# Three modulation blocks moved to an earlier layer, two last taps and two group roots set ahead of weight splits, and small matrix products given other places

## The chip, the cores and the metric

The kernel runs on one core of one Trainium2 chip. The metric is the device time of one execution in microseconds (us). TensorE is called PE below, VectorE DVE, ScalarE ACT, GpSimd POOL and SyncE SP. Each engine takes its instructions strictly in the order in which they were written into its program, and waits at each one until the semaphores that it names have come.

## The reference

A two-layer "macaron" network with adaptive norms, one batch, 256 tokens, width 1024, all in float32. There are six sub-layers: feed-forward, hybrid mixer, feed-forward, then feed-forward, mLSTM, feed-forward. The change touches the first two. Each sub-layer gets a modulation (shift, scale and gate) that is a product of one conditioning vector with a large matrix:

```python
for layer in range(DEPTH):
    mod = (c_act @ ada_w[layer] + ada_b[layer]).reshape(bsz, N_SUB, 3, D_MODEL)[:, :, :, None, :]
    def modulate(t, sub):
        return rms_norm(t, norm_g[layer, sub]) * (1.0 + mod[:, sub, 1]) + mod[:, sub, 0]
    h = modulate(x, 0)
    x = x + HALF_STEP * (1.0 + mod[:, 0, 2]) * swiglu(h, ffn_w_gate[layer, 0], ...)
    h = modulate(x, 1)
    y = hybrid_mixer(h, ...)          # layer 0; layer 1 has the mLSTM here
    x = x + (1.0 + mod[:, 1, 2]) * y
    ...

def hybrid_mixer(h, w_in, w_out, ...):
    gate_lru, x_lru, z_ssd, xbc, dt_raw = jnp.split(h @ w_in, HYB_SPLITS, axis=-1)
    x_lru = causal_conv(x_lru, lru_conv_w, lru_conv_b)            # 4 taps
    y_lru = rg_lru(x_lru, ...) * jax.nn.gelu(gate_lru)
    xbc = jax.nn.silu(causal_conv(xbc, ssd_conv_w, ssd_conv_b))   # 4 taps
    ...
    y = ssd_chunked(xs, dt, a, bm, cm) + ssd_d[:, None] * xs
    y = y * jax.nn.silu(z_ssd)
    y = rms_norm(y in 2 groups of 512, ssd_norm_g)
    return jnp.concatenate([y_lru, y], axis=-1) @ w_out
```

## The kernel before, in words

**Weights in pieces.** All weight matrices stream through the core as one list of 128x128 tiles, eight to a piece of 512 KB. For each piece SP issues one DMA into one of four raw buffers (`wraw`, line 95). ACT rounds the piece to a high part (`whi`, line 101), and DVE subtracts that from the raw piece to get the low part (`wlo`, line 102, called the split below). PE then makes three products of each tile (high by high, high by low, low by high; lines 443 to 445, or 509 to 511 at the start of a sub-layer), 24 to a piece. These products are called stream products. The first feed-forward takes pieces 0 to 65, the hybrid mixer pieces 66 to 119, and four more sub-layers follow. Places within the hybrid are counted in stream products from piece 66 on: "at 788" means behind 788 of them.

**Modulation blocks.** The modulation of all sub-layers is 144 blocks of 512 KB (`ada`, line 262). Each is a DMA into one of three buffers and one multiply-and-accumulate on DVE. `ADA_PLAN` says in which sub-layer, and over which of its pieces, a range of blocks is spread evenly; 24 blocks belong to each sub-layer, in the order of the sub-layers, so blocks 24 to 47 are the hybrid's (40 to 47 its gate, used at its end).

**What sets the order.** The text of the program is written sub-layer by sub-layer. A list scheduler that works with costs of its own decides at build time in which order each engine gets its instructions, within the data dependencies and the buffer counts. Extra edges without a wait bind its choice: `W.behind(i, n, ins)` puts the ACT cast (n = 0) or the DVE split (n = 1) of piece i behind an instruction; `stand(ins, s, n)` puts a small PE product behind stream product n of sub-layer s; `in_one_go` ties products to each other; `issue_after` keeps everything in a block behind an instruction.

**The norm ahead of the hybrid (called n1).** Each 128-row slice of x is finished on DVE (line 571), squared on ACT (line 416), and the squares are summed over the rows by small PE products (`rst_n1`, line 359, at 11). DVE takes the reciprocal root in nine instructions on 128x2 numbers (`rsv`, `rsy`, `rsw`, lines 373 and 320 to 329), and two PE products spread it over all rows (`rsb_n1`, line 405, at 28). The first stream products of the sub-layer run on unnormalised rows meanwhile.

**The hybrid's own work.** Convolutions are one ACT instruction and three DVE taps (line 733), on `ssd_x` (from PE's `xbc`) and on `lru_x` (from PE's `xl`). Each `lru_x` slice is then split into a high part by ACT (line 426) and a low part by DVE (line 427), for the gate products `ri`. For each of four pairs of heads PE writes decay rows (`ab`, line 974), ACT makes from them `mt` (lines 983 and 986) and `ce` (line 985), DVE multiplies both with other matrices (lines 988 and 992), and PE makes y0, y2, y4 and y6 (line 1008). DVE and ACT scale and square y; after y2 and after y6 a group norm runs like the one above (`rst_g`, `rsv_g` to `rsy_g`, `rsb_g`; groups 0 and 1), and its result `ysb` is the input of the out products `od`. The `lru` scan (lines 1055 and 1057 on DVE) waits on a square root (line 1051) on ACT.

## Time and profile before

| what | value |
|---|---|
| three timed runs | 1096.56, 1097.56 and 1098.46 us (median 1097.56) |
| the profiled execution's own time | 1097.25 us |
| its span | 1095.5 us, so that 1.75 us lie around it |
| PE busy | 1083.8 us (99%) |
| DVE busy | 920.5 us (84%) |
| ACT busy | 639.5 us (58%) |
| DMA | 272.34 MB, mean 249 GB/s |
| first feed-forward | from the start to 193.7 us |
| hybrid | 193.7 to 367 us |

The rows of the timeline give start, duration, engine, line, operation, tiles out<-in and shapes, and in brackets the engine's idle time before the row with what ended it. A matmul's duration overlaps the next one's, so PE's pace is read from the distance of starts. Names in the rows leave out the buffer numbers.

### The profile page before, as it was taken

Reading aid. Unit: us, or ns where it says so; the run is one execution under the profiler, and the core shown is the slowest. Engines: PE = TensorE matmul, PEld = TensorE weight load, DVE = VectorE, ACT = ScalarE, POOL = GpSimd, SP = SyncE. Lnnn points to the kernel's source line nnn. Section 1 sums busy time; section 2 is a strip of 40 time slices with the busy share of each in tenths; the row PEclk is TensorE's granted clock in tenths of the full one; section 3 lists DMA queues with packets and bytes.
Section 4 is the critical chain, followed back from the end, with each engine's and each line's share of the span. In section 5 each row is a group of like instructions: output and inputs, shape, how many; then the busy total and the mean of one; then the engine's idle time right before and its main releaser. Section 6 shows DMA issues by size and latency. Waiting matters only on the chain.

```text
span 1095.5 us, 23272 instructions
## 1 busy us (share of the span) xinstructions
PE 1083.8 (99%) x9315; PEld 1070.4 (98%) x9315; DVE 920.5 (84%) x1654; ACT 639.5 (58%) x1053; POOL 8.8 (1%) x28
## 2 busy tenths in 40 slices
PE   9999999999999999999999999999999999999997
PEld 7999999999999999999999999999999999999997
DVE  7999999899999899989698798979768868866552
ACT  5765555678986564554454455448776655544452
POOL 0000000000000000000000000010000000000000
PEclk9999999999999999999999999999999999999999
DMA  9889999556855489999848799963432664875551
GB/s 375 344 318 391 387 352 343 178 196 195 279 167 191 139 307 370 354 351 327 281 142 323 266 356 346 338 204 119 146 102 81 208 193 137 298 239 193 193 174 39
DMA packets 75534, 272.34 MB, mean 249 GB/s; under 512 B 8593, under 2 KB 9393, under 8 KB 75426
## 3 DMA queue, kind: packets, MB, share of 16 engines
q1 hardware_dynamic: 74592, 269.38, 69.7%
q8 instruction: 73, 1.20, 0.4%
q0 software_dynamic: 400, 1.04, 0.4%
q10 hardware_dynamic: 434, 0.43, 0.1%
q14 instruction: 35, 0.29, 0.1%
HBM read 269.77 MB, written 1.05 MB: 247 GB/s over the span
## 4 chain that ended last, share of the span: by engine, by line
PE 80%; DVE 12%; DMA 4%; issue 2%; ACT 1%; ACTq 0%; DVEq 0%; SPq 0%
PE gu L445 12%; PE gu L444 12%; PE gu L443 11%; PE od L445 10%; PE od L443 10%; PE od L444 10%; DVE wlo L102 4%; DMA wraw<-in_wst_dram 3%; PE zz L445 1%; PE zz L443 1%; PE zz L444 1%; DMA wgr<-in_ml_wg_dram 1%; DVE ada L262 1%; DVE xc L733 1%; PE gu_f L509 1%
## 5 line engine op out<-in xcount | busy, mean ns | idle before, releaser
L102 DVE TENSOR_TENSOR wlo<-wraw,whi 128x1024 fp32r<-128x1024 f32 x364 | 442.9, 1221 | 83.6 <-ACT whi L101 83.0
L101 ACT CAST whi<-wraw 128x1024 fp32r<-128x1024 f32 x364 | 378.2, 1050 | 210.9 <-DMA wraw<-in_wst_dram 80.2
L444 PE MATMUL gu<-hb,whi 128*128 128x256 f32 x1296 | 358.0, 276 | 0.4 <-DVE hb L668 0.3
L443 PE MATMUL gu<-hb,whi 128*128 128x256 f32 x1296 | 358.0, 276 | 0.0
L445 PE MATMUL gu<-hb,wlo 128*128 128x256 f32 x1296 | 357.9, 276 | 0.1
L444 PEld LDWEIGHTS gu<-hb,whi 128*128 128x128 f32 x1296 | 243.3, 188 | 0.8 <-DVE hb L668 0.8
L445 PEld LDWEIGHTS gu<-hb,wlo 128*128 128x128 f32 x1296 | 243.3, 188 | 0.2 <-DVE wlo L102 0.2
L443 PEld LDWEIGHTS gu<-hb,whi 128*128 128x128 f32 x1296 | 243.2, 188 | 0.0
L443 PE MATMUL od<-ph,whi 128*128 128x256 f32 x704 | 194.3, 276 | 0.0
L444 PE MATMUL od<-ph,whi 128*128 128x256 f32 x704 | 194.3, 276 | 0.0
L445 PE MATMUL od<-ph,wlo 128*128 128x256 f32 x704 | 194.3, 276 | 0.0
L262 DVE SCALAR_TENSOR_TENSOR ada<-ada,cact 128x1024 f32<-128x1024 f32 x144 | 175.3, 1218 | 1.4 <-DMA ada<-in_adaT_dram 1.3
L444 PEld LDWEIGHTS od<-ph,whi 128*128 128x128 f32 x704 | 132.1, 188 | 0.0
L445 PEld LDWEIGHTS od<-ph,wlo 128*128 128x128 f32 x704 | 132.1, 188 | 0.0
L443 PEld LDWEIGHTS od<-ph,whi 128*128 128x128 f32 x704 | 132.1, 188 | 0.0
L426 ACT CAST ph<-fg 128x256 fp32r<-128x256 f32 x88 | 35.1, 406 | 114.9 <-DVE fg L595 114.9
L427 DVE TENSOR_TENSOR ph<-fg,ph 128x256 fp32r<-128x256 f32 x88 | 36.4, 421 | 14.2 <-ACT ph L426 14.2
L416 ACT ACTIVATE sq_o<-x 128x256 f32<-128x256 f32 x42 | 17.5, 418 | 45.6 <-DVE x L571 40.6
L571 DVE SCALAR_TENSOR_TENSOR x<-od,gate,x 128x256 f32<-128x256 f32 x48 | 23.1, 481 | 24.4 <-PE od L445 24.2
L444 PE MATMUL zz<-hb,whi 128*128 128x256 f32 x128 | 36.2, 283 | 0.0
L445 PE MATMUL zz<-hb,wlo 128*128 128x256 f32 x128 | 36.1, 282 | 0.0
L443 PE MATMUL zz<-hb,whi 128*128 128x256 f32 x128 | 35.8, 279 | 0.0
(431 smaller groups left out, 1959.1 us busy)
## 6 DMA issues: line engine op xcount, KB each, us to landing
wraw<-in_wst_dram SPq DMA_DIRECT2D x366, 512.0 KB, 4.6
ada<-in_adaT_dram SPq DMA_DIRECT2D x144, 512.0 KB, 5.6
xn<-in_x_dram SPq DMA_DIRECT2D x2, 512.0 KB, 4.0
wgr<-in_ml_wg_dram POOLq DMA_DIRECT2D x3, 256.0 KB, 5.4
...
```

Of the source, the lines that this page charges most:

```text
L101: raw_hi = nc.scalar.copy(hi, raw)
L102: self.last = nc.vector.tensor_tensor(out=lo, in0=raw, in1=hi.bitcast(F32), op=ALU.subtract)
L262: return nc.vector.scalar_tensor_tensor(out=raw, in0=raw, scalar=1.0, in1=cact, op0=ALU.mult, op1=ALU.mult, accum_out=mods[s][:, m:m + 1])
L416: square = nc.scalar.activation(q, x, AF.Square).ins
L426: nc.scalar.copy(hi, src)
L427: nc.vector.tensor_tensor(out=both[:, 1, :], in0=src, in1=hi.bitcast(F32), op=ALU.subtract)
L443: m = nc.tensor.matmul(dst, wh, both[:, 0, :], start=start, stop=False, skip_group_check=True)
L444: W.products += [m, nc.tensor.matmul(dst, wh, both[:, 1, :], start=False, stop=False, skip_group_check=True), nc.tensor.matmul(dst, wl, bo ...
L445: nc.tensor.matmul(dst, wl, both[:, 0, :], start=False, stop=stop, skip_group_check=True)]
L509: W.products += [nc.tensor.matmul(dst, wh, rh, start=(k == 0), stop=False), nc.tensor.matmul(dst, wh, rl, start=False, stop=False), nc.ten ...
L571: nc.vector.scalar_tensor_tensor(out=xs_t[d], in0=dst, scalar=g[:, d:d + 1], in1=xs_t[d], op0=ALU.mult, op1=ALU.add)
L733: nc.vector.scalar_tensor_tensor(out=dst[:, o:], in0=src[:, :T - o], scalar=cw(j), in1=dst[:, o:], op0=ALU.mult, op1=ALU.add)
```

## The change

The edits are these. (1) `ADA_PLAN`: blocks 40, 41 and 42 move from the hybrid to the first feed-forward, where blocks 16 and 17 now come at pieces 14 and 15, and blocks 18 to 42 (25 instead of 24) from piece 17 to 43; the hybrid keeps blocks 43 to 47, spread over its pieces 22 to 34. (2) The last tap of the first `ssd_x` slice is set ahead of the split of piece 75, and the last tap of the last `lru_x` slice ahead of the split of piece 97. (3) The end of the reciprocal root of group 0 is set ahead of the split of piece 105, that of group 1 ahead of that of piece 109; the scans come behind the root of group 1; the splits into `ysb0` to `ysb3` are written right behind group 0's norm. (4) y0 and y2 get places at 788 and 797, the sums of group 1 at 948 and their spread at 976; the n1 spread's place at 28 is written down, and 48 stream products are held behind the n1 sums and the n1 spread. No instruction is added or removed.

```diff
-SUMS = {"n1": (1, 11), "n2": (2, 11), "n4": (4, 14)}
+SUMS = {"n1": (1, 11), "n2": (2, 11), "n4": (4, 14), "g1": (1, 948)}
+KEPT, HELD = ("n1",), 48
+SPREADS = {"n1": (1, 28), "n2": (2, 28), "g1": (1, 976)}
...
 ADA_PLAN = [
-    (0, (17, 43), range(16, 40)), (0, (43, 65), range(48, 64)), (1, (22, 37), range(40, 48)),
+    (0, (14, 16), range(16, 18)), (0, (17, 43), range(18, 43)), (0, (43, 65), range(48, 64)),
+    (1, (22, 34), range(43, 48)),
     (2, (6, 60), range(64, 104)), (3, (6, 60), range(104, 136)), (5, (6, 40), range(136, 144)),
...
+    def hold(ins, s, n):
+
+        holds.append((ins, 3 * PIECE * starts[s] + n))
...
             if nm in SUMS:
                 stand(products[0], *SUMS[nm])
+                if nm in KEPT:
+                    hold(products[-1], *SUMS[nm])
...
-            if nm == "n2" and b == 0:
-                stand(m, 2, 28)
+            if b == 0 and nm in SPREADS:
+                stand(m, *SPREADS[nm])
+            if b == 1 and nm in KEPT:
+                hold(m, *SPREADS[nm])
...
+    taps = []
+
     def conv(dst, src, cw, cb, i, n):
...
-            nc.vector.scalar_tensor_tensor(out=dst[:, o:], in0=src[:, :T - o], scalar=cw(j), in1=dst[:, o:],
-                                           op0=ALU.mult, op1=ALU.add)
+            taps.append(nc.vector.scalar_tensor_tensor(out=dst[:, o:], in0=src[:, :T - o], scalar=cw(j),
+                                                       in1=dst[:, o:], op0=ALU.mult, op1=ALU.add))
...
                 xbc(xs[:, i, :], b[:, 0:T], i)
+                if i == 0:
+                    W.behind(starts[1] + 9, 1, taps[-1])
...
                 conv(xl[:, c, :], b[:, 0:T], lambda j: col("lru_cw", 8 * j + c), col("lru_cb", c), c, 8)
+                if c == 7:
+                    W.behind(starts[1] + 31, 1, taps[-1])
...
             in_one_go(products, needed)
+            if m0 < 4:
+                stand(products[0], 1, (788, 797)[m0 // 2])
...
                 if g == 0:
                     group_norm(0)
-        ys = [sp.tile([P, 2, T], F32R, tag=f"ssd{m % 4}{m // 4}", name=f"ysb{m}") for m in range(8)]
-        for m in range(4):
-            split(xs[:, m, :], ys[m])
+                W.behind(starts[1] + (39, 43)[g], 1, rsqrt_ends[-1])
+                ys += [sp.tile([P, 2, T], F32R, tag=f"ssd{m}{g}", name=f"ysb{4 * g + m}") for m in range(4)]
+                if g == 0:
+                    for m in range(4):
+                        split(xs[:, m, :], ys[m])
+        second_root = rsqrt_ends[-1]
...
-                nc.vector.tensor_tensor_scan(out=xl[:, c, :], data0=av[:, c, :], data1=nq[:, c, :], initial=0.0,
-                                             op0=ALU.mult, op1=ALU.add)
+                with tc.issue_after(second_root.ins):
+                    nc.vector.tensor_tensor_scan(out=xl[:, c, :], data0=av[:, c, :], data1=nq[:, c, :], initial=0.0,
+                                                 op0=ALU.mult, op1=ALU.add)
...
+    for i, n in holds:
+        for m in W.products[n:n + HELD]:
+            tc.add_manual_dep(m.ins, i.ins.name, NOSYNC, reason="not later")
```

The scheduler puts more in other places than the diff names. Three places follow, first of the kernel before, then of the changed one. In the changed kernel's rows the same source lines have numbers that are higher by 3 to 21. Numbers behind a name tell pieces and buffers (`wlo68` is piece 68); the last number is a serial one.

DVE where the first feed-forward ends and the hybrid begins, kernel before: `od0_7` is the last out product's bank, `rst_n1` the sum of the squares.

```order
L290 SCALAR_TENSOR_TENSOR scale2_4845<-scale2_4845,cols_104 128x8 [waits DVE_49]
L102 TENSOR_TENSOR wlo68_2546<-wraw68_2543,whi68_2545 128x1024 [waits DMAHW2_49,Activation_49]
L102 TENSOR_TENSOR wlo69_2576<-wraw69_2573,whi69_2575 128x1024 [waits DMAHW3_49,PE_49,Activation_49]
L571 SCALAR_TENSOR_TENSOR x_103<-od0_7_2524,gate0_1931,x_103 128x256 [waits PE_49]
L831 TENSOR_SCALAR dt_3168<-cols_104 128x8
L490 SCALAR_TENSOR_TENSOR hb_106<-x_103,scale1_1937,hb_106 128x256 [waits DVE_49,Activation_49]
L373 TENSOR_SCALAR rsv_n1_2636<-rst_n1_2631 128x2 [waits PE_49]
L320 TENSOR_SCALAR rsy_n1_2639<-rsv_n1_2636 128x2 [waits DVE_49]
...
L329 SCALAR_TENSOR_TENSOR rsy_n1_2639<-rsw_n1_2638,rsy_n1_2639 128x2 [waits DVE_49]
L102 TENSOR_TENSOR wlo70_2659<-wraw70_2656,whi70_2658 128x1024 [waits DMAHW4_49]
```

The same place in the changed kernel:

```order
L582 SCALAR_TENSOR_TENSOR x_103<-od0_7_2533,gate0_1940,x_103 128x256 [waits PE_49]
L846 TENSOR_SCALAR dt_3177<-cols_104 128x8
L292 TENSOR_TENSOR scale2_4845<-mod2_1814,cols_104 128x8 [waits DVE_49]
L293 SCALAR_TENSOR_TENSOR scale2_4845<-scale2_4845,cols_104 128x8 [waits DVE_49]
L105 TENSOR_TENSOR wlo68_2555<-wraw68_2552,whi68_2554 128x1024 [waits DMAHW5_49,Activation_49]
L501 SCALAR_TENSOR_TENSOR hb_106<-x_103,scale1_1946,hb_106 128x256 [waits Activation_49]
L382 TENSOR_SCALAR rsv_n1_2645<-rst_n1_2640 128x2 [waits PE_49]
L105 TENSOR_TENSOR wlo69_2585<-wraw69_2582,whi69_2584 128x1024 [waits DMAHW6_49,Activation_49]
L327 TENSOR_SCALAR rsy_n1_2648<-rsv_n1_2645 128x2 [waits DVE_49]
...
L336 SCALAR_TENSOR_TENSOR rsy_n1_2648<-rsw_n1_2647,rsy_n1_2648 128x2 [waits DVE_49]
L105 TENSOR_TENSOR wlo70_2668<-wraw70_2665,whi70_2667 128x1024 [waits DMAHW7_49,Activation_49]
```

The splits of pieces 68 and 69 stood ahead of the last x; now they stand behind it, one ahead of the last `hb` and one between the first and the second instruction of the n1 root.

DVE at the last taps on `lru_x` (slice 7, shapes 128x255, 128x254, 128x253), kernel before:

```order
L102 TENSOR_TENSOR wlo96_3815<-wraw96_3812,whi96_3814 128x1024 [waits DMAHW1_49,PE_49]
L733 SCALAR_TENSOR_TENSOR lru_x_2628<-xl7_3793,cols_104,lru_x_2628 128x255 [waits Activation_49]
L102 TENSOR_TENSOR wlo97_3853<-wraw97_3850,whi97_3852 128x1024 [waits DMAHW3_49,PE_49]
L733 SCALAR_TENSOR_TENSOR lru_x_2628<-xl7_3793,cols_104,lru_x_2628 128x254 [waits DVE_49]
L262 SCALAR_TENSOR_TENSOR ada43_3856,mod1_1153<-ada43_3856,cact_117 128x1024 [waits DMAHW2_49]
L733 SCALAR_TENSOR_TENSOR lru_x_2628<-xl7_3793,cols_104,lru_x_2628 128x253 [waits DVE_49]
...
L427 TENSOR_TENSOR xlb7_3828<-lru_x_2628,xlb7_3828 128x256 [waits Activation_49]
```

and the changed one:

```order
L265 SCALAR_TENSOR_TENSOR ada45_3824,mod1_1086<-ada45_3824,cact_117 128x1024
L746 SCALAR_TENSOR_TENSOR lru_x_2637<-xl7_3799,cols_104,lru_x_2637 128x255 [waits Activation_49]
L1070 TENSOR_SCALAR lru_aq_2638<-lru_aq_2638 128x1024
L746 SCALAR_TENSOR_TENSOR lru_x_2637<-xl7_3799,cols_104,lru_x_2637 128x254 [waits DVE_49]
L967 SCALAR_TENSOR_TENSOR ssd_z_2636<-ssd_z_2636,z5_3840 128x256 [waits Activation_49]
L746 SCALAR_TENSOR_TENSOR lru_x_2637<-xl7_3799,cols_104,lru_x_2637 128x253 [waits DVE_49]
L105 TENSOR_TENSOR wlo97_3862<-wraw97_3859,whi97_3861 128x1024 [waits DMAHW6_49,PE_49]
L438 TENSOR_TENSOR xlb7_3837<-lru_x_2637,xlb7_3837 128x256 [waits Activation_49]
```

The split of piece 97 and a modulation block stood between the taps; now a 128x1024 instruction (line 1070, which was line 1050 and came later) and one on `ssd_z` stand there. On ACT, at the cast of that slice (`xlb7`), before:

```order
L926 ACTIVATE lru_aq_2629<-lru_aq_2629,hc_3198 128x256 [waits Activation_49]
L927 ACTIVATE lru_aq_2629<-lru_aq_2629,hc_3198 128x256 [waits Activation_49]
L101 CAST whi99_3941<-wraw99_3939 128x1024 [waits DMAHW6_49,PE_49]
L426 CAST xlb7_3828<-lru_x_2628 128x256 [waits DVE_49]
L929 ACTIVATE a2_5_3880<-lru_aq_2629 128x256 [waits Activation_49]
L949 ACTIVATE ssd_z_2627<-z6_3883 128x256 [waits PE_49]
```

and now:

```order
L941 ACTIVATE lru_aq_2638<-lru_aq_2638,hc_3207 128x256 [waits Activation_49]
L437 CAST xlb7_3837<-lru_x_2637 128x256 [waits DVE_49]
L942 ACTIVATE lru_aq_2638<-lru_aq_2638,hc_3207 128x256 [waits Activation_49]
L104 CAST whi99_3947<-wraw99_3945 128x1024 [waits DMAHW1_49,PE_49]
L944 ACTIVATE a2_5_3886<-lru_aq_2638 128x256 [waits Activation_49]
L966 ACTIVATE ssd_z_2636<-z6_3889 128x256 [waits PE_49]
```

The cast of `xlb7`, which waits for the last tap, stood behind two other instructions and now stands ahead of them.

DVE at the root of group 1, kernel before:

```order
L373 TENSOR_SCALAR rsv_g1_4436<-rst_g1_4431 128x2 [waits PE_49]
L102 TENSOR_TENSOR wlo109_4523<-wraw109_4520,whi109_4522 128x1024 [waits DMAHW5_49]
L320 TENSOR_SCALAR rsy_g1_4439<-rsv_g1_4436 128x2 [waits DVE_49]
L1055 SCALAR_TENSOR_TENSOR lru_aq_2629<-lru_x_2628,lru_aq_2629 128x1024 [waits Activation_49]
L323 TENSOR_TENSOR rsw_g1_4438<-rsy_g1_4439 128x2 [waits DVE_49]
L1055 SCALAR_TENSOR_TENSOR lru_aq_2629<-lru_x_2628,lru_aq_2629 128x1024 [waits Activation_49]
L324 SCALAR_TENSOR_TENSOR rsw_g1_4438<-rsw_g1_4438,rsv_g1_4436 128x2 [waits DVE_49]
L1057 SCALAR_TENSOR_TENSOR lru_x_2628<-lru_aq_2629 128x256
...
L1057 SCALAR_TENSOR_TENSOR lru_x_2628<-lru_aq_2629 128x256
L329 SCALAR_TENSOR_TENSOR rsy_g1_4439<-rsw_g1_4438,rsy_g1_4439 128x2 [waits DVE_49]
L102 TENSOR_TENSOR wlo110_4557<-wraw110_4554,whi110_4556 128x1024 [waits DMAHW7_49,PE_49,Activation_49]
L963 SCALAR_TENSOR_TENSOR ssd_x_2626<-ssd_x_2626,cols_104,rsb_g1_4490 128x256 [waits PE_49]
```

and the changed one, from the middle of the root (ahead of it the first five instructions of the root follow each other) to the low parts of `ysb4` to `ysb7`:

```order
L1075 SCALAR_TENSOR_TENSOR lru_aq_2638<-lru_x_2637,lru_aq_2638 128x1024 [waits Activation_49]
L333 SCALAR_TENSOR_TENSOR rsy_g1_4451<-rsw_g1_4450,rsy_g1_4451 128x2 [waits DVE_49]
L1075 SCALAR_TENSOR_TENSOR lru_aq_2638<-lru_x_2637,lru_aq_2638 128x1024 [waits Activation_49]
L334 TENSOR_TENSOR rsw_g1_4450<-rsy_g1_4451 128x2 [waits DVE_49]
L335 SCALAR_TENSOR_TENSOR rsw_g1_4450<-rsw_g1_4450,rsv_g1_4448 128x2 [waits DVE_49]
L336 SCALAR_TENSOR_TENSOR rsy_g1_4451<-rsw_g1_4450,rsy_g1_4451 128x2 [waits DVE_49]
L1078 SCALAR_TENSOR_TENSOR lru_x_2637<-lru_aq_2638 128x256 x3
L980 SCALAR_TENSOR_TENSOR ssd_x_2635<-ssd_x_2635,cols_104,rsb_g1_4490 128x256 [waits PE_49]
L980 SCALAR_TENSOR_TENSOR ssd_x_2635<-ssd_x_2635,cols_104,rsb_g1_4490 128x256 x3
...
L438 TENSOR_TENSOR ysb6_4462<-ssd_x_2635,ysb6_4462 128x256 [waits Activation_49]
L105 TENSOR_TENSOR wlo109_4523<-wraw109_4520,whi109_4522 128x1024 [waits DMAHW6_49]
L438 TENSOR_TENSOR ysb7_4463<-ssd_x_2635,ysb7_4463 128x256 [waits Activation_49]
```

The splits of pieces 109 and 110 and all but three of the scans have left the stretch between the first instruction of the root and the scaling by `rsb_g1`; three scans stand between the root's end and that scaling, and the split of piece 109 between the low parts of `ysb6` and `ysb7`. On PE, by the count of stream products, y0 goes from 778 to 788, y2 from 808 to 807, the sums and the spread of group 0 from 847 and 896 to 840 and 859, y4 from 868 to 896, y6 from 901 to 912, and the sums and the spread of group 1 from 931 and 987 to 948 and 979.

6 lines of the change are left out of this document (3 added, 3 removed).

## The prediction

> **What bounds the kernel now.** I read the page first, then the waits of PE between 194 and 367 us (the hybrid), then windows of the span, then the timeline at each wait. The page says that PE sets the time:
>
> ```profile
> PE 1083.8 (99%) x9315; PEld 1070.4 (98%) x9315; DVE 920.5 (84%) x1654; ACT 639.5 (58%) x1053; POOL 8.8 (1%) x28
> ```
>
> No product is removed, so a gain can only come out of PE's stalls. In the hybrid the list of waits names four (engine and line, what was waited for, us, times, longest):
>
> ```profile
> PE y L1008 <- DVE mt L988: 0.8, 1, 0.8
> PE z L443 <- DVE lru_x L733: 0.8, 1, 0.8
> PE rsb_g L405 <- DVE rsy_g L329: 0.7, 1, 0.7
> PE xbc L443 <- DVE ssd_x L733: 0.3, 1, 0.3
> ```
>
> Their sum, 2.6 us, is too small, since the idle time counts only after the modelled end of the product before. In a stretch without stalls 241 products take 27 us, 0.113 us each from start to start (first row below, with its count); the second shows PE's and DVE's busy time in a late stretch of the hybrid:
>
> ```profile
> 101.00:128.00 27.00, 27.00 (x241) 27.00 (x240) 26.97 (x43) 13.56 (x21) 0.00 (x0) 1.00 1.00 382
> 260.00:287.00 27.00, 26.23 (x225) 25.55 (x224) 26.94 (x52) 22.40 (x44) 0.00 (x0) 1.00 0.73 248
> ```
>
> So a stall is the distance of two starts less 0.113:
>
> ```profile
> 220.24 0.28 PE L445 MATMUL xbc<-hb,wlo 128*128 128x256 f32 x1
> 220.79 0.36 PE L443 MATMUL xbc<-hb,whi 128*128 128x256 f32 x1 [0.28 <-DVE ssd_x L733]
> ...
> 282.85 0.28 PE L445 MATMUL ri<-xlb,wlo 128*128 128x256 f32 x1
> 283.90 0.39 PE L443 MATMUL z<-hb,whi 128*128 128x256 f32 x1 [0.77 <-DVE lru_x L733]
> ...
> 293.41 0.97 PE L974 MATMUL ab<-stk,sel 128*128 128x256 f32 x4
> 294.22 0.28 PE L443 MATMUL gl<-hb,whi 128*128 128x256 f32 x1
> ...
> 295.28 0.28 PE L443 MATMUL gl<-hb,whi 128*128 128x256 f32 x1
> 296.41 0.66 PE L1008 MATMUL y<-mt,ssd 128*64 128x128 f32 x8 [0.85 <-DVE mt L988]
> ...
> 330.61 0.28 PE L445 MATMUL od<-ysb,wlo 128*128 128x256 f32 x1
> 331.61 0.68 PE L405 MATMUL rsb_g<-ident,rsy_g 128*128 128x128 f32 x4 [0.72 <-DVE rsy_g L329]
> ```
>
> That gives 0.44 us at the `xbc` product, 0.94 at z7, 1.02 at y0 and 0.89 at group 1's spread. The `ab` products take 0.81 us for four that at 0.113 would take 0.45, so 0.35 more. In all 3.6 us can be had, 0.3% of the time, if nothing new waits. DVE is as full as PE (26.94 of 27 us), so what is set ahead on it sets something else back.
>
> **FFN: three more blocks (about 0).** A block costs DVE 1.14 us from start to start (the `ada` row at 282.22 below, next start 283.37) and 0.524 MB of DMA, at the 382 GB/s of the window above 1.37 us. The two blocks at pieces 14 and 15 meet these rows, where DVE idles for 2.17 us before it reaches the split of piece 20, whose first PE use follows in the last row:
>
> ```profile
> 59.43 1.23 DVE L102 TENSOR_TENSOR wlo<-wraw,whi 128x1024 fp32r<-128x1024 f32 x1 [0.79 <-ACT whi L101]
> ...
> 64.02 1.77 DVE L427 TENSOR_TENSOR ph<-fg,ph 128x256 fp32r<-128x256 f32 x5 [1.38 <-ACT ph L426]
> ...
> 66.04 1.22 DVE L102 TENSOR_TENSOR wlo<-wraw,whi 128x1024 fp32r<-128x1024 f32 x1
> ...
> 68.81 0.28 PE L445 MATMUL gu<-hb,wlo 128*128 128x256 f32 x1
> ```
>
> The split ends at 67.26 and has 1.55 us to spare. Two blocks and one more small subtraction ahead of it (0.33) are 2.6 us against 2.17 of idle time: the split is at most 0.5 late, still in time. Later the DMA engines are full (share 1.00), and the one block more from piece 17 to 43 takes 1.37 us there; I take the 1.55 us as the room of the pieces behind it too. I take 0, bounds 0 and +1.4 (one full transfer). The Trainium skill (Perfetto Trace Analysis, Roofline) puts the ceiling of 16 DMA engines at about 435 GB/s, by which the block would cost an estimated 1.2 us; the trace disagrees, since the share there is 1.00 at 382. The sum does not change by it.
>
> **The n1 root (+1.2).** This speaks against the change. Before, the splits of pieces 68 and 69 are done ahead of the last x, and DVE then idles:
>
> ```profile
> 190.19 2.36 DVE L102 TENSOR_TENSOR wlo<-wraw,whi 128x1024 fp32r<-128x1024 f32 x2
> 193.91 0.48 DVE L571 SCALAR_TENSOR_TENSOR x<-od,gate,x 128x256 f32<-128x256 f32 x1 [1.36 <-PE od L445]
> ...
> 195.34 0.48 DVE L490 SCALAR_TENSOR_TENSOR hb<-x,scale,hb 128x256 fp32r<-128x256 f32 x1 [0.87 <-ACT hb L489]
> 196.05 0.16 DVE L373 TENSOR_SCALAR rsv_n<-rst_n 128x2 f32<-128x2 f32 x1 [0.23 <-PE rst_n L359]
> ...
> 197.62 0.16 DVE L329 SCALAR_TENSOR_TENSOR rsy_n<-rsw_n,rsy_n 128x2 f32<-128x2 f32 x1
> ```
>
> and PE takes the spread 0.23 us after the root's end at 197.78, at its usual pace, so without room:
>
> ```profile
> 198.01 0.61 PE L405 MATMUL rsb_n<-ident,rsy_n 128*128 128x128 f32 x4
> ```
>
> Now the first split starts behind x and the scales at about 194.7 and ends at 195.9, so `hb` starts 0.5 us later and `rsv` at about 196.2, 0.1 to 0.2 late (it had waited 0.23); then the second split adds 1.14 us. The root ends 1.2 to 1.3 us later, and the spread keeps its place at 28, with 48 products held behind it, so PE waits: +1.2 (bounds +1.1 and +1.4; 0 only if PE had room that the row does not show). What waits behind the spread is all of PE; the pieces' splits have room.
>
> **Taps and the chain behind them (-0.4).** DVE rows of before, then ACT's, and one DVE row that waits:
>
> ```profile
> 280.70 1.21 DVE L102 TENSOR_TENSOR wlo<-wraw,whi 128x1024 fp32r<-128x1024 f32 x1
> ...
> 282.22 1.22 DVE L262 SCALAR_TENSOR_TENSOR ada<-ada,cact 128x1024 f32<-128x1024 f32 x1
> ...
> 283.37 0.48 DVE L733 SCALAR_TENSOR_TENSOR lru_x<-xl,cols,lru_x 128x253 f32<-128x253 f32 x1
> ```
>
> ```profile
> 283.88 0.41 ACT L426 CAST xlb<-lru_x 128x256 fp32r<-128x256 f32 x1 [0.23 <-DVE lru_x L733]
> ...
> 293.37 0.46 ACT L985 ACTIVATE ce<-ab 128x256 f32<-128x256 f32 x1
> ```
>
> ```profile
> 234.55 1.26 DVE L733 SCALAR_TENSOR_TENSOR ssd_x<-xbc,cols,ssd_x 128x255 f32<-128x255 f32 x3 [1.25 <-ACT ssd_x L730]
> ```
>
> At `xbc` the tap moves ahead of one split, 1.14 us, more than the stall of 0.44 and its echo of 0.08 in the next step: -0.5. PE is then 0.7 us late against before (1.2 less 0.5), and DVE too, since at 234.55 it waits for PE's product by way of ACT. At z7 the tap passes a split and a block (2.28 us) and gets 0.93 of other work ahead of it: 1.35 earlier, more than the stall, so PE gains 0.94 and 0.1 of echo. But the cast of `xlb7` on ACT now stands ahead of two instructions that were done while it waited, so ACT comes no earlier into the stretch from 283.88 to 293.6, where it has no idle time and whose end (`ce`) frees the bank for the `ab` products. PE's gain of 1.05 us at z7 comes back there, with 0.1 more. Together -0.4 (bounds -1.55, if ACT comes earlier, and -0.1).
>
> **Places of y0 and y2 (-0.7).** y0 stands ten products (1.1 us) later, its stall was 1.02 with 0.1 of echo: -1.1. Then y2 follows 19 products (2.2 us) behind it instead of 30. DVE must first finish `ce`, take y0's result (two instructions) and then make mt2, which has the shape of a split (1.14 us), behind the ACT row below. The first two rows are DVE's groups of the hybrid, busy time and mean ns:
>
> ```profile
> L1012 DVE SCALAR_TENSOR_TENSOR ssd_x<-ssd_x,cols,y 128x256 f32<-128x256 f32 x8 | 3.6, 477 | 0.5 <-PE y L1008 0.4
> L992 DVE TENSOR_TENSOR ce<-ce,ssd 128x512 f32<-128x512 f32 x4 | 2.7, 687 | 0.2 <-ACT ce L985 0.2
> ```
>
> ```profile
> 298.09 1.19 ACT L986 ACTIVATE mt<-mt 128x1024 f32<-128x1024 f32 x1
> ```
>
> From y0's end the two (0.8 to 0.95), mt2 (1.14) and the hand-overs make 2.3 to 2.6 us, against 2.2: 0.1 to 0.4, and the ACT row, itself some 0.8 late by the ACT chain, ends at 300.1 and can add to it. I take +0.4 (0 to 0.9).
>
> **Both group roots (+0.9).** Group 0's spread stands 19 products (2.2 us) behind the sums; the nine small instructions take 1.73 us (196.05 to 197.78) and one of line 992 (0.6 to 0.69) stands between them, 2.4 with the hand-over: +0.3 (0 to 0.9). For group 1 the splits leave the root, but two 1.14 us instructions stay, and these wait for ACT's square root behind a table load:
>
> ```profile
> 323.04 1.28 ACT L1051 ACT_TABLE_LOAD   x1
> 324.34 2.01 ACT L1051 ACTIVATE lru_aq<-lru_aq 128x1024 f32<-128x1024 f32 x2
> ```
>
> From the squares to the second square root's end are 0.5, 1.3 and 1.9 us, then 1.14 and 0.6 to the root's end, 5.4 in all; PE comes to the spread after the last addition on DVE (0.7), the sums (0.45, like the `ab` group) and 31 products (3.5), 4.7 behind the squares. The wait is 0.7 to 1.2, the old one was 0.89: +0.1 (-0.9 to +0.5). The Trainium skill (ScalarE: Activation LUTs, What ACT_TABLE_LOAD costs) adds a drain of about 1.38 us to each such load; by that the estimate would be 1.4 more, but here the next instruction starts 1.30 us after the load's start, so the trace shows no drain. Behind the root, three scans and the split of piece 109 now stand ahead of parts of this work:
>
> ```profile
> 332.52 1.65 DVE L963 SCALAR_TENSOR_TENSOR ssd_x<-ssd_x,cols,rsb_g 128x256 f32<-128x256 f32 x4
> 334.08 1.42 DVE L427 TENSOR_TENSOR ysb<-ssd_x,ysb 128x256 fp32r<-128x256 f32 x4
> ```
>
> `ysb7` comes 1.14 us later, and PE wants it about 1 us after `ysb4`: +0.5 (0 to 0.9).
>
> **The sum.** 0 + 1.2 - 0.4 - 0.7 + 0.3 + 0.1 + 0.5 = +1.0 us. On the profiled execution, 1097.25 (span 1095.5 and 1.75 around it), that is 1098.3; it lies 0.3 under the median of the runs shown, so the median becomes 1098.6. All the low bounds give 1.2 - 1.55 - 1.1 - 0.9 = -2.4, all the high ones +4.8.
>
> **The rivals.** (a) All the old waits go and only the n1 root waits, ACT following the tap: -2.4, 1095.2; with no wait there either -3.6, 1094.0. For it: each moved instruction passes more work than its stall was long. Against it: ACT's full stretch behind 283.88. (b) Slower: the splits put off at the end of the feed-forward hold the n1 root, and the compressed chain y0, y2, group 0's root and `ysb7` waits at each link in full (0.9 + 0.9 + 0.9): it decides from the point where DVE's chain from y0 is longer than PE's distance; 1.2 - 0.4 - 1.1 + 0.9 + 0.9 + 0.5 + 0.9 = +2.9, 1100.5. For it: DVE is full; against it: the split buffers have room. (c) The waits only change places, since DVE or ACT is the true limit of the hybrid: +0, 1097.6. For it: 26.94 of 27 us.
>
> **How the numbers follow.** Forecast 0.45, (a) 0.22, (b) 0.18, (c) 0.15. A measurement of this kernel can tell about 0.2%, 2.2 us, from no change. Faster by more than that (under 1095.4) is most of (a) and a bit of the rest: 0.22. Slower (over 1099.8) is nearly all of (b) and some of the forecast's upper end: 0.24. Within: 0.54. The range, 1094.9 to 1100.9, leaves out the deep end of (a) and more than (b); the forecast's own range is 1097.2 to 1100.2.
>
> **What would show it.** After the change the list of PE's waits should have the `rsb_n` product of n1 at about 198 with 1.0 to 1.3 us, no `xbc` and no z wait, a longer `ab` (1.4 us or more over 0.45), no y0 wait, group 1's spread still waiting, and a wait at `ysb7`. If `rsb_n` does not wait there, or `ab` keeps its 0.8, I am wrong towards (a); if PE stalls before 190 us, the feed-forward term is.

## The result, and the profile after

The changed kernel takes 1104.52 us (median of 6 runs, 1102.63 to 1105.57) against 1097.26 of the kernel before: 1.0063 times as long, 95% interval 1.0050 to 1.0076. It is slower by 7.3 us, where 1.0 was predicted and the range ended at 1100.9. Four executions of 1555 to 2875 us (one of the kernel before, two of no_plan_no_g1_edge, one of before_all_mild) were slow ones, and the medians, ratios and counts below are of the others.

In the two profiled executions (1102.98 and 1097.25) the spans differ by 5.7 us. The waits of PE between 120 and 380 us in the changed kernel (engine and line, what was waited for, us, times, longest) answer to the four of before:

```profile
PE rst_n L366 <- ACT sq_o L427: 1.7, 1, 1.7
PE od L454 <- ACT ssd_z L1046: 1.0, 1, 1.0
PE ab L991 <- ACT ce L1002: 1.0, 2, 0.8
PE rsb_n L414 <- DVE rsy_n L336: 0.8, 1, 0.8
PE y L1025 <- DVE mt L1005: 0.6, 1, 0.6
PE y L1025 <- DVE ssd_x L1031: 0.3, 1, 0.3
PE od L455 <- DVE ysb L438: 0.3, 1, 0.3
PE rsb_g L414 <- DVE rsy_g L336: 0.3, 1, 0.3
```

`xbc`, z7 and y0 are gone, as the change meant. New are the n1 spread, a longer `ab`, y2, y6, the first `od` product, `ysb`, and at the top the sums of the norm behind the hybrid (`rst_n` of n2, line 366). PE's rows at the ends of six of these waits:

```profile
200.81 0.60 PE L414 MATMUL rsb_n<-ident,rsy_n 128*128 128x128 f32 x3 [0.83 <-DVE rsy_n L336]
...
296.62 0.50 PE L991 MATMUL ab<-stk,sel 128*128 128x256 f32 x2 [0.80 <-ACT ce L1002]
...
322.60 0.66 PE L1025 MATMUL y<-mt,ssd 128*64 128x128 f32 x8 [0.32 <-DVE ssd_x L1031]
...
325.16 0.38 PE L454 MATMUL od<-ysb,whi 128*128 128x256 f32 x1 [1.03 <-ACT ssd_z L1046]
...
339.98 0.38 PE L455 MATMUL od<-ysb,whi 128*128 128x256 f32 x1 [0.32 <-DVE ysb L438]
...
374.57 0.61 PE L366 MATMUL rst_n<-ones,sq_o 128*128 128x1 f32 x4 [1.68 <-ACT sq_o L427]
```

I laid the starts of the same stream products in the two traces side by side; the difference grows at these places (us, after less before, each to about 0.1):

| place | predicted | measured |
|---|---|---|
| first 36 us, same instructions | - | +1.2 |
| `od` at 150.4 (FFN blocks) | 0 | +0.4 |
| n1 sums and spread | +1.2 | +1.3 |
| `xbc` | -0.5 | -0.55 |
| z7, then `ab` | -1.05, +1.15 | -0.85, +1.2 |
| y0, then y2 | -1.1, +0.4 | -0.95, +0.65 |
| group 0's sums and spread | +0.3 | +0.55 |
| y6 | not seen | +0.5 |
| first `od` product, for its bank | not seen | +1.0 |
| group 1's sums and spread | +0.1 | -0.85 |
| `ysb7` | +0.5 | +0.65 |
| n2 sums | not seen | +1.8 |
| near 616 | - | -0.35 |

That is 5.7 with the first row and 4.5 without it. The first row is no part of the change: the other profiles below begin alike, and there the same place stands 0 to 1.1 us later than in the kernel before.

The second view is the table of windows from 300 to 354 us: us, then the busy time of PE, PEld, DVE, ACT and POOL, the granted clock, DMA share and GB/s. First the kernel before:

```profile
300.00:310.00 10.00, 10.00 (x98) 9.69 (x98) 9.94 (x17) 8.20 (x21) 0.00 (x0) 1.00 0.63 209
...
326.00:334.00 8.00, 7.28 (x65) 7.11 (x64) 8.00 (x19) 7.21 (x11) 0.00 (x0) 1.00 0.39 126
334.00:340.00 6.00, 6.00 (x56) 6.00 (x55) 6.00 (x11) 3.59 (x6) 0.00 (x0) 1.00 0.35 117
```

and the changed kernel, with one window more:

```profile
300.00:310.00 10.00, 9.32 (x99) 8.61 (x93) 7.63 (x11) 8.52 (x21) 0.00 (x0) 1.00 0.47 145
310.00:320.00 10.00, 9.92 (x96) 9.62 (x96) 8.71 (x22) 8.59 (x23) 0.00 (x0) 1.00 0.22 73
...
326.00:334.00 8.00, 7.99 (x71) 7.79 (x69) 4.88 (x14) 7.14 (x9) 0.00 (x0) 1.00 0.23 84
334.00:340.00 6.00, 5.40 (x46) 5.23 (x46) 6.00 (x14) 4.81 (x10) 0.00 (x0) 1.00 0.00 0
```

DVE was never idle between 326 and 334 us; now it is idle for 3.1 us there and for 2.4 between 300 and 310. From 334 to 340 not one byte of DMA moves (0 GB/s). The DVE rows that wait, from the timeline of the changed kernel, and at the end the first x of the hybrid (of od1_0):

```profile
301.10 0.69 DVE L1009 TENSOR_TENSOR ce<-ce,ssd 128x512 f32<-128x512 f32 x1 [1.19 <-ACT ce L1002]
...
309.18 0.69 DVE L1041 TENSOR_TENSOR gacc<-gacc,sq 128x512 f32<-128x512 f32 x1 [1.15 <-ACT sq L1040]
311.02 0.16 DVE L382 TENSOR_SCALAR rsv_g<-rst_g 128x2 f32<-128x2 f32 x1 [1.15 <-PE rst_g L366]
...
327.47 0.69 DVE L1041 TENSOR_TENSOR gacc<-gacc,sq 128x512 f32<-128x512 f32 x1 [0.70 <-ACT sq L1040]
330.38 0.16 DVE L382 TENSOR_SCALAR rsv_g<-rst_g 128x2 f32<-128x2 f32 x1 [2.22 <-PE rst_g L366]
...
360.01 0.48 DVE L582 SCALAR_TENSOR_TENSOR x<-od,gate,x 128x256 f32<-128x256 f32 x1
```

Five waits, 6.4 us: the first (1.19) for ACT's `ce`, the other four (5.2) for the hand-overs of the two groups' roots to ACT and PE. In the kernel before splits and modulation blocks stood in these gaps (two blocks at 302.34 and 307.89, which the new plan no longer has there). The splits now follow behind the root; the raw buffers that they would free stay full (no weight DMA is issued from 326.2 to 339.7; the kernel before has gaps of 10.9 and 6.8 us between 313.5 and 332.6), and x starts at 360.01 instead of

```profile
353.21 0.48 DVE L571 SCALAR_TENSOR_TENSOR x<-od,gate,x 128x256 f32<-128x256 f32 x1
```

PE's own products are 4.2 us later there (351.5 against 347.2 for the same product). Of the other 2.6, 1.8 are left when ACT's last square ends (374.52 against 368.46), and that is what PE waits for at n2.

### The profile page after: what moved, and what is told of

It is laid out like the page before. It is cut to its first block, busy times and chain, and to the rows that moved or that the text cites. A ratio compares the mean times of both kernels' runs of the same rounds, so it can differ in the third digit from the quotient of the medians.

```text
span 1101.2 us, 23272 instructions
## 1 busy us (share of the span) xinstructions
PE 1085.5 (99%) x9315; PEld 1071.4 (97%) x9315; DVE 921.4 (84%) x1654; ACT 638.3 (58%) x1053; POOL 8.7 (1%) x28
## 3 DMA queue, kind: packets, MB, share of 16 engines
HBM read 269.77 MB, written 1.05 MB: 246 GB/s over the span
## 4 chain that ended last, share of the span: by engine, by line
PE 77%; DVE 13%; ACT 4%; DMA 4%; issue 2%; ACTq 0%; DVEq 0%; SPq 0%
PE gu L456 13%; PE gu L455 13%; PE gu L454 13%; PE od L456 8%; PE od L454 8%; PE od L455 8%; DVE wlo L105 4%; DMA wraw<-in_wst_dram 3%; ACT whi L104 1%; PE zz L454 1%; PE zz L456 1%; PE zz L455 1%; PE gu_f L522 1%; PE gu_f L520 1%; PE gu_f L521 1%
## 5 line engine op out<-in xcount | busy, mean ns | idle before, releaser
L438 DVE TENSOR_TENSOR ph<-fg,ph 128x256 fp32r<-128x256 f32 x88 | 36.4, 421 | 13.5 <-ACT ph L437 13.4
L605 ACT ACTIVATE fg<-gu 128x256 f32<-128x256 f32 x82 | 30.6, 376 | 13.2 <-PE gu L456 13.1
L455 PE MATMUL zz<-hb,whi 128*128 128x256 f32 x128 | 36.2, 283 | 0.0
```

The lines of the kernel that those rows point to most:

```text
L438: nc.vector.tensor_tensor(out=both[:, 1, :], in0=src, in1=hi.bitcast(F32), op=ALU.subtract)
L455: W.products += [m, nc.tensor.matmul(dst, wh, both[:, 1, :], start=False, stop=False, skip_group_check=True), nc.tensor.matmul(dst, wl, bo ...
L605: nc.scalar.activation(g, b[:, 0:T], AF.Silu)
```

## The experiments

Each was timed in five or more executions beside the kernel before on the same chip; "1.0045 [1.0030, 1.0061]" is its ratio to that kernel with the 95% interval.

### Parts of the changed kernel undone

**The split inside the n1 root.** One edge in the begin of the hybrid:

```diff
             W.behind(i0 + (4 if s < 3 else 6), 1, rsqrt_ends[-1])
+            if s == 1:
+                W.behind(i0 + 3, 1, rsqrt_ends[-1])
```

> The changed kernel with one more edge: the split of piece 69, which stood inside the first norm's root (n1) in it, stands behind the root. Theory (each wait of PE is a term of its own): PE's product `rsb_n` at about 200 us, 1.12 us from its predecessor in the changed kernel, follows at its usual pace, and the whole is about 1.0 us shorter, 1103.5 against 1104.5; the wait of `rst_n` at the second norm stays at 1.7. Rival (waits only change places, since DVE is full behind that place): the time given free is taken by the `y`, `od` or `rst_n` products later, and the whole stays at 1104.5 within 0.4.

Measured 1102.17 us, 1.0045 [1.0030, 1.0061]. The wait at n1 is gone and the one at `ab` is halved, 1.7 us by the starts of the products. But its list of PE's waits shows where they went:

```profile
PE rst_n L366 <- ACT sq_o L427: 2.7, 1, 2.7
```

One us came back at n2. The two windows over that place show something else (the granted clock is the third number from the end, 0.63):

```profile
370.00:374.00 4.00, 1.33 (x11) 1.21 (x10) 2.56 (x7) 2.10 (x6) 0.18 (x1) 0.94 0.59 204
374.00:378.00 4.00, 4.00 (x23) 4.00 (x24) 2.59 (x10) 0.01 (x1) 0.00 (x0) 0.63 0.04 10
```

So the rival holds for more than half of it by the wait alone. Behind the longer wait PE ran at a lower clock, which neither theory had, and with it the profiled execution lost all of the 1.7 again and 0.8 more. The six executions lie between 1100.55 and 1106.04, too far apart to tell more from their median.

**The first x ahead of a split.** `W.behind(starts[2] - 1, 1, made)`, with `made` the first x:

> The changed kernel with one more edge: the split of piece 119 on DVE stands behind the first x (of od1_0) at the end of the hybrid. Theory (the second norm's sums wait 1.7 us because that x starts only at 360.0, behind a split that itself waits for its piece, though PE is done with od1_0 at about 357.5): x starts 1 to 1.9 us earlier and the chain x, squares, sums behind it too, so the wait of `rst_n` falls from 1.7 to between 0 and 0.8 and the whole by 0.9 to 1.7 us, to about 1103.2. Rival (the chain is paced by DVE's 2.26 us for each slice and by the splits of pieces 120 to 123, which come with their DMAs): the first x is earlier, the last is not, and `rst_n` waits as long as before, 1104.5.

Measured 1102.38 us, 1.0038 [1.0025, 1.0051]. The wait at n2 fell only to

```profile
PE rst_n L366 <- ACT sq_o L427: 1.1, 1, 1.1
```

by 0.6, less than the theory's least: the later slices of x, 2.26 us apart on DVE, set the last one. In the profiled execution the clock fell here too (0.61 from 374 to 378).

**Without the edge at group 1's root.**

```diff
-                W.behind(starts[1] + (39, 43)[g], 1, rsqrt_ends[-1])
+                if g == 0:
+                    W.behind(starts[1] + 39, 1, rsqrt_ends[-1])
```

> The changed kernel without the one edge that puts the split of piece 109 behind the root of group 1: pieces 109 to 111 are split ahead of or inside that root. Theory (the edge keeps raw buffers full, so that no weight DMA is issued from 326.2 to 339.7 us, the pieces behind come late and with them the first x, the second norm's sums and PE): the gap in the DMA issues closes to 6 us or less, the wait of `rst_n` (1.7) disappears, the spread of group 1 (0.46 over its pace) and `ysb` may wait up to 1 us more; the whole falls by 0.7 to 1.9 us, to 1102.6 to 1103.8. Rival (the gap in the issues is caused by the ACT and DVE work of the hybrid's end and not by this edge): the gap and the wait of `rst_n` stay, 1104.5 or more.

Measured 1101.65 us, 1.0035 [1.0023, 1.0047], less than the theory's range. The wait at n2 is gone, though the gap in the issues did not close: two of 6.9 and 9.4 us (326.8 to 333.7, 334.9 to 344.3) stand in place of one of 13.5. And group 1's spread and `ysb` wait about 1.4 us more: by the starts of the products, without the first 36 us, PE is only 0.5 us earlier than in the changed kernel. The median is 2.9 lower, and all executions kept their clock (mean 0.998 to 0.999; the changed kernel's six have 0.995 to 0.998), which I take for the greater part of it.

**The copies ahead of a square on ACT**, so that the bank of the first `od` product comes free earlier (`tc.add_manual_dep(squares.ins, copied.ins.name, ...)` for `gl5`):

> The changed kernel with one more edge on ACT: the copies of the `gl4` and `gl5` banks (0.5 us), which stood behind the square of the third pair and so waited for DVE's `ssd_x`, stand ahead of it. Theory (the first `od` product waits 1.03 us for the bank that these copies free): that wait disappears and PE comes 1.2 us earlier into the out products; group 1's root does not wait for this bank, so up to 0.6 of it returns at its spread; the whole falls by 0.6 to 1.2 us, to about 1103.6. Rival (group 1's root sets the pace there and takes all of it): the spread of group 1 waits 1.2 us longer, and the whole stays at 1104.5 within 0.3.

Measured 1104.76 us, 1.0060 [1.0048, 1.0072]: no gain. The bank's wait fell by half, and

```profile
PE rst_n L366 <- ACT sq_o L427: 2.4, 1, 2.4
```

took it, with a clock of 0.50 behind it from 374 to 378. The rival was right that something later takes all of it, but it is n2 and not the spread.

**Without the new plan and that edge** (taps, places and early roots stay):

> The changed kernel with the old plan of the modulation blocks and without the edge of the split of piece 109: the taps, the places of y0 and y2, both early roots' other edges and the scans' are left. Theory (the n1 root's 1.1 us and the second norm's 1.7 us with the clock behind it are two thirds of the loss): neither of the two waits is there, the mean clock is 0.998 to 0.999, and the whole is at 1099.5 to 1101. Rival (other waits of the hybrid, at the `y`, `od` and `ysb` products, take what these two give back): 1102 or more.

Measured 1100.45 us, 1.0026 [1.0016, 1.0035]. Neither wait is there, and 4.1 of the 7.3 us are gone. Of the rest, PE waits 1.5 us for group 1's `ysb`, right behind 0.7 at its spread. Behind these waits the clock fell, 0.78 in the mean of this window:

```profile
334.00:340.00 6.00, 4.45 (x25) 4.05 (x25) 6.00 (x15) 3.78 (x8) 0.00 (x0) 0.78 0.28 89
```

That cost some 1.5 more. Five of the eight executions have a mean clock of 0.996 or 0.997, where the theory had 0.998 to 0.999. So the clock does not fall at n2 alone. The wait for the first `od` product's bank is gone as well, though y0 and y2 keep their new places: y6 stands at 915 here, behind the first three `od` products.

### What a wait of PE costs

**Waits on purpose.** In the kernel before, n2's sums and spread were given earlier places, which nothing else needs (the diff leaves out that 48 stream products are held behind each, as at n1 in the change):

```diff
-SUMS = {"n1": (1, 11), "n2": (2, 11), "n4": (4, 14)}
+SUMS = {"n1": (1, 11), "n2": (2, 1), "n4": (4, 14)}
...
-                stand(m, 2, 28)
+                stand(m, 2, 8)
```

> The kernel before with nothing changed but the places of two groups of small products at the second norm (n2): its sums at 1 instead of 11 and its spread at 8 instead of 28, so that PE waits there on purpose (in the kernel before the sums follow ACT's last square by 0.05 us and the spread the sums by 3.05). Theory (a wait of PE costs its own length and nothing else): 10 products of 0.113 us fewer cover the sums and 13 fewer the root, so PE waits about 1.1 and 1.3 us, and the whole is 2.4 us longer, 1100.3 against 1097.9, in all executions alike, at the same mean granted clock of 0.999. Rival (two waits of this length also bring TensorE's granted clock down for some us, as the windows behind the same place showed in two of the last four profiles, 0.50 to 0.63 over 4 us): 1 to 4 us more than that, 1101 to 1104, a lower mean clock (0.995 to 0.998), and executions that differ by some us.

Measured 1102.92 us, 1.0042 [1.0028, 1.0056]. One execution kept its clock (0.999) and took 1099.27, about the sum of the waits; the other five took 1102.61 to 1103.66 (0.995 to 0.998). The profiled one waits 1.5 and 1.1 us:

```profile
PE rst_n L359 <- ACT sq_o L420: 1.5, 1, 1.5
PE rsb_n L407 <- DVE rsy_n L329: 1.1, 1, 1.1
```

and up to 376.1 its products follow each other in 0.214 us, where the kernel before has 0.12 for the same ones (of 258 columns):

```profile
374.23 0.42 PE L513 MATMUL gu_f<-hb,whi 128*128 128x258 f32 x1
374.45 0.42 PE L514 MATMUL gu_f<-hb,whi 128*128 128x258 f32 x1
374.66 0.42 PE L515 MATMUL gu_f<-hb,wlo 128*128 128x258 f32 x1
```

The rival is right: the waits cost 2 us themselves, and the executions with a lower clock take 3.3 to 4.4 more.

**Half of that**, the sums at 1 and the spread left at 28:

> The kernel before with the second norm's sums at 1 instead of 11 and its spread left at 28: half of the earlier run's wait on purpose. Theory (a single wait of about 1.1 us is already long enough to lower the clock in some executions): the wait is 1.1 us; executions without a fall of the clock take 1098.5, those with it about 2 to 3 more, and the median lies between 1099 and 1101. Rival (only the two waits together did it): 1098.5 in all executions, mean clock 0.999.

Measured 1099.54 us against 1097.9, 1.0015 [1.0006, 1.0024]; single executions from 1097.87 to 1102.03, clocks 0.996 to 0.999. In the profiled execution the wait is 1.4 us and the clock does not fall. Three of the eleven have a mean clock of 0.997 or less, as one of 92 of the kernel before has, so a single wait lowers the clock in some executions.

### The bound behind group 1's root

**A split made twice.** In the kernel before, piece 113's subtraction is issued a second time:

```diff
+            if i == 113:
+                self.last = nc.vector.tensor_tensor(out=lo, in0=raw, in1=hi.bitcast(F32), op=ALU.subtract)
```

> The kernel before in which the split of piece 113 on DVE (1.14 us from start to start) is made twice, the second time over the first with the same numbers; the order on PE is unchanged. Theory (from the group's root to the first x DVE is without idle time, so its work there is the second bound of the hybrid, and the second norm's sums, which follow ACT's last square by 0.05 us, have no room): the first x starts 1.0 to 1.2 us later than 353.2, PE waits about 1.0 to 1.1 us at the second norm's sums, and the whole is 1.0 to 1.2 us longer in an execution without a fall of the granted clock, some 2 us more where it falls, 1098.5 to 1100.5 in the median. Rival (the pieces' DMAs or PE's own out products pace the first x, and a split more is hidden): no wait there, 1097.5 within 0.3.

Measured 1098.5 us against 1097.9, 1.0012 [1.0003, 1.0021]. In the profiled execution the wait is there, as long as the split:

```profile
PE rst_n L361 <- ACT sq_o L418: 1.1, 1, 1.1
```

It fell to a clock of 0.70 behind it and lost another 1.6:

```profile
370.00:374.00 4.00, 4.00 (x27) 4.00 (x27) 3.07 (x11) 0.10 (x1) 0.00 (x0) 0.70 0.14 51
374.00:378.00 4.00, 4.00 (x31) 4.00 (x31) 2.55 (x6) 1.58 (x4) 0.00 (x0) 0.88 0.37 131
```

So in this execution DVE's work from the root to x has no room: what is added there, PE waits for at n2. The first x came 2.0 us later (355.20), more than expected, since DVE also waited 1.2 for an ACT cast; the last square ends 1.25 later. The seven executions without a fall of the clock (0.998 and more) take 1097.8 to 1098.6, 0.4 more than the kernel before in the median, so in the timed executions some room may be left.

### Parts of the change done alone

**The edge at group 1's root**, on the kernel before:

```diff
                 if g == 0:
                     group_norm(0)
+                else:
+                    W.behind(starts[1] + 43, 1, rsqrt_ends[-1])
```

> The kernel before with one edge of the change: the split of piece 109 behind the root of group 1. Theory (this edge alone fills the raw buffers): SP issues no weight DMA for 8 us or more around 326 to 338, the splits of pieces 113 to 119 follow their DMAs, the first x at the hybrid's end comes at least 1 us later than 353.2, and the sums at the second norm wait 1 to 2.5 us; group 1's spread waits up to 0.9 less; the whole 0.5 to 2 us longer, and more where the clock falls: 1098.5 to 1101.5. Rival (the gap needs the later y products and the later root that the whole change brings): no gap over 7 us, no wait at the second norm, 1097.5 within 0.4.

Measured 1099.36 us against 1097.47, 1.0012 [1.0004, 1.0021]. The spread's 0.7 is gone and n2's sums wait 1.2; the profiled execution kept its clock and is as long as before (span 1095.5). Three executions take 1097.2 to 1097.6 (mean clock 0.998 to 0.999), eight 1098.7 to 1099.9 (0.997 to 0.998): the waits only change places, and the clock, as I read it, makes the loss. The gaps in the issues are those of the kernel before (10.9 and 6.6 us, there 10.9 and 6.8), so the rival was right that this edge alone opens none, and wrong on the wait; the first x starts at 354.18, 1.0 later than before, as the theory had it.

**The taps alone**:

> The kernel before with the two edges of the last taps alone. Theory (as predicted, ACT's full stretch behind the cast of `xlb7` sets the `ab` products): the waits of `xbc` (0.44) and z7 (0.94) go, the second pair of `ab` products waits about 1.0 more, the whole 0.3 to 0.5 us shorter, 1097.4. Rival (ACT follows the tap): 1.4 to 1.5 us shorter, 1096.4, and `ab` as before.

Measured 1097.7 us against 1097.47, 1.0002 [0.9994, 1.0011]. z7 comes 1.05 earlier and `ab` gives 1.2 back, at

```profile
293.99 0.50 PE L980 MATMUL ab<-stk,sel 128*128 128x256 f32 x2 [0.81 <-ACT ce L991]
```

as predicted; `xbc`, z7 and `ab` net to about -0.2, which the times can't show.

**The plan alone**:

> The kernel before with the new plan of the modulation blocks alone. Theory (the n1 root is late for the reason predicted, splits put off by the added blocks, and a single wait of about 1 us does not lower the clock): PE's spread at about 200 us stands 1.1 us behind its predecessor, nothing before 190 us waits more than 0.4, the later waits of the kernel before stay, the mean clock is 0.999, and the whole is 0.9 to 1.5 us longer, 1098.7. Rival (the later sub-layers win from three blocks fewer in the hybrid what n1 loses): 1097.5 within 0.4.

Measured 1102.87 us, 1.0047 [1.0034, 1.0060], far more than either theory. Its waits begin with

```profile
PE rst_n L360 <- ACT sq_o L417: 1.9, 1, 1.9
PE xbc L444 <- DVE ssd_x L734: 1.7, 1, 1.7
```

There is no wait at n1 at all. Nothing holds the spread at 28 in this kernel, so it stands later, and the same lateness of DVE is paid at `xbc`, 1.6 us more than in the kernel before, instead of 1.3 at n1. And n2 waits without the edge at group 1's root, with a gap of 12.2 us in the weight DMAs (326.7 to 338.9) that no edge of the roots has made. The blocks that left the hybrid leave DVE idle between 300 and 320 (2.4 us against 0.8); that this makes what follows late is my reading, and no run shows it by itself.

**Both early roots and the scans alone**:

> The kernel before with both groups' roots ahead of the splits and the scans behind group 1's root, nothing else of the change. Theory (the early roots themselves bring the waits that I had not foreseen): the wait of the second norm's sums is there (1 to 2 us, with a falling clock in most executions), and so are waits at the y6 and the first `od` product of about 1 us in all, because y6 and the group's sums come later by the places that the list gives them (915 and 963 for 901 and 931); 1100 to 1102. Rival (only together with the places of y0 and y2 do y4, y6 and `od` wait): no wait at y6 and `od` over 0.3, only the second norm's; 1098.5 to 1099.8.

Measured 1102.64 us, 1.0044 [1.0030, 1.0058]: n2's sums wait 2.6 us, `od` for `ysb` 0.6; y6 and the first `od` product do not wait for more than 0.3, as the rival had it. But n2, with a fall of the clock behind it that cost 1.6 in the profiled execution, takes the time past the theory's range all the same.

### Versions meant to be faster

**The root free, the splits in their turn**: in the kernel before, the products and scans of the `lru` stand behind group 1's root and, both of them, behind the split of piece 110, and the spread stands at 972:

> A version meant to be faster than the kernel before: that kernel with group 1's root kept free of the square roots' products and scans on DVE (they stand behind the root, the scans also behind the split of piece 110), while the splits of pieces 109 and 110 keep their turn, and the spread of group 1 at 972. Theory (what was right in the change is the root, what was wrong is the splits put off): the spread's 0.89 falls to 0 to 0.2, no weight DMA waits for more than in the kernel before, the second norm's sums do not wait, the clock stays at 0.999: 0.5 to 0.9 us shorter, 1096.8. Rival (DVE is full there, so the scans put off make `ylb` and the pieces behind late): a wait at the second norm of 0.5 us or more takes it back, 1097.5 or more.

Measured 1098.76 us, 1.0009 [1.0000, 1.0018]. The spread's wait is gone (PE is 1.0 us earlier behind it) and n2's sums wait 1.3. Seven executions with a mean clock of 0.997 take 1098.7 to 1099.6, the four with 0.998 or 0.999 take 1096.9 to 1097.9. With the places of y0 and y2:

> The run before with the places of y0 and y2 of the change (788 and 797) as well. Theory (each place's wait is a term of its own as long as no split is put off): y0's 1.02 goes, y2 waits 0.4 to 0.8, so a further 0.2 to 0.6 us shorter, 1096.4. Rival (y2's wait takes all of y0's gain): equal to the run before, 1096.8 within 0.3.

1098.85 us, 1.0012 [1.0003, 1.0021]: y2 took most of what y0 gave (0.3 us are left behind it), and n2's sums wait 1.4.

**With the first x ahead of the split of piece 119**:

> The run before_root_scans with the first x at the hybrid's end ahead of the split of piece 119 as well, meant to be faster than the kernel before. Theory (PE won about 1.3 us at group 1's spread there and lost it at the second norm, because the first x stood behind a split that follows its DMA): x comes 1 to 2 us earlier, the wait of 1.3 falls to 0.3 to 0.7, the clock does not fall, 1096.6 to 1097.2. Rival (the splits of pieces 120 to 123 pace the later x, as when this edge was put into the changed kernel, where the wait fell by only 0.6): 0.7 us or more of wait, and no gain, 1097.4 or more.

Measured 1097.06 us against 1097.9, 0.9994 [0.9985, 1.0003]: the wait at n2 fell to 0.4, the clock kept at 0.998 to 0.999, and the span is 0.7 us shorter. This is the one version that keeps a part of the gain, and it can't be told from the kernel before.

**With the `xbc` tap and y0 and y2 at 788 and 812**:

> The run before_root_x with the `xbc` tap's edge and with y0 at 788 and y2 at 812 (five products later than in the change): the parts of the change that put off no split. Theory (each removes a wait of its own and PE and DVE shift together): `xbc` 0.4, y0 and y2 0.6 to 0.9 shorter, on top of the run before_root_x, so 1095.8 to 1096.3. Rival (DVE's full stretch up to the first x does not become shorter by PE's earlier products, so the second norm's sums wait by as much as PE wins, with the clock behind it): 1097.4 to 1099.5.

1098.71 us, 1.0008 [0.9999, 1.0017]. n2's sums wait only 0.4, but y6 and group 0's spread moved to 904 in the order, and z7 waits 1.2, a `gu` product 0.6, `ysb` 0.5 and group 1's sums 0.4. The time lies in the rival's range, but neither theory had these waits.

## Why the prediction was wrong

**What held.** Most terms of the sum came within 0.3 us of what was measured: n1 (+1.2, +1.3), `xbc`, z7 given back at `ab`, y0, y2 within its bounds, group 0's spread, `ysb7`. before_taps shows `xbc`, z7 and `ab` by themselves. The FFN term, taken as 0, was 0.4 (and the 382 GB/s from which its upper bound came are no ceiling: the kernel before moves 408 from 30 to 42 us). Group 1's sums and spread won 0.85 where +0.1 was taken (within the bound of -0.9). Against the sum of +1.0 the two traces differ by 4.5 without the first row. Of the 3.5 that the sum lacks, n2 is 1.8, y6 and the bank are 1.5, and the rest nearly cancels. The median adds 1.5 to the profiled execution, which I put down to the clock.

**The step that failed first: "What waits behind the spread is all of PE; the pieces' splits have room", said at n1 and again against rival (b), and carried over to the groups' roots.** I costed what a root gains when the splits leave it, and asked of the splits only whether PE needs them in time. They had that room. But they were also what DVE did while a root waited for ACT and PE. With them behind it, and with three modulation blocks fewer, DVE is idle for 6.4 us and then full from 334 to 354, the raw buffers stay full, and the first x is 6.8 us later, 2.6 more than PE. That n2 consumes all this I did not ask, and the sum has no term for it; it cost 1.8. In the kernel before ACT's last square ends at 368.47 and PE's sums start 0.05 us later, two rows of the timeline that I had not read:

```profile
368.05 0.42 ACT L416 ACTIVATE sq_o<-x 128x256 f32<-128x256 f32 x1 [1.03 <-DVE x L571]
```

```profile
368.52 0.60 PE L359 MATMUL rst_n<-ones,sq_o 128*128 128x1 f32 x4
```

before_roots shows it without the new plan: four DVE waits of 1.1 to 1.3 us at the roots' hand-overs, 4.7 in all, and a first x 3.5 us later (356.74). before_split_twice shows that its profiled execution had no room, before_g1_edge and before_roots that the roots' part of the change alone brings this wait, before_plan that the plan brings it too.

**The second: rival (c), the waits only change places, had 0.15.** For the hybrid's end it is the right reading: n1_one_split, copies_first, before_g1_edge and before_root_scans each took 1.0 to 1.7 us of waits away and found more than half or all of it at n2. PE and DVE arrive there together, so neither can win alone. The +0 of that rival is not what came, since n2, y6 and the bank are new waits. I had the row for it (DVE busy 26.94 of 27 us), but used it as an argument, not as a term.

**The third: a wait was priced at its own length.** In the profiled execution of the changed kernel the clock stays at 1.00 behind n2, and its span shows the waits alone:

```profile
374.00:378.00 4.00, 3.43 (x30) 3.43 (x30) 2.55 (x12) 0.81 (x2) 0.00 (x0) 1.00 0.19 70
```

The six timed executions have mean clocks of 0.995 to 0.998 and are 1.5 us longer in the median. g1_no_edge has nearly as much waiting (0.5 us less by the starts) but none of its waits is longer than 1.03 us, and its median is 2.9 us lower. The Trainium skill (TensorE: Matmul & The Clock Gate, HAM oscillation) gives the rule that PE must not idle for more than about 3.4 us; by it none of these waits would cost clock. The measurement decides otherwise: 1.1 us were enough in the profiled execution of before_split_twice. The statement in the same page (What's actually happening) that the window runs freely fits executions of one kernel that differ by 3 us, though no run here shows the window itself.

**The fourth: y4 and y6.** The change moves y4 from 868 to 896 and y6 from 901 to 912, right ahead of the first `od` product. The order of instructions showed this and I gave it no term; it cost 0.5 at y6 and 1.0 at the bank. The bank's wait is there in every kernel that has y6 right ahead of the first `od` product (g1_no_edge too, which lacks the edge at group 1's root) and not in before_roots and no_plan_no_g1_edge, where y6 stands three `od` products later. The latter has the new places of y0 and y2, so these do not bring it by themselves; which other part puts y6 there was not tried alone. copies_first says that halving this wait gains nothing while n2 waits.

**The n1 root.** The size was right, the cause only in part. before_plan shows that the lateness is DVE's and comes with the plan; that the hold at 28 chooses the place where it is paid fits the two orders and was not tried alone.

What stays open: why before_plan loses 1.6 us at `xbc` where the whole change loses 1.3 at n1 (the tap's edge, which the whole change has, may be the difference; it was not tried), and when a wait lowers the clock. The kernel before waits 0.8 us at y0, and one of 92 executions has a mean clock of 0.997 or less. With one wait of 1.1 to 1.4 us at n2 it is 3 to 7 of eleven (before_sums_early, before_split_twice, before_g1_edge, before_root_scans and its version with y0 and y2), but with 1.2 us at z7 one of ten (before_all_mild).
